# Second gate unit: second-column weight tiles split two tiles ahead into the large pool, with the first nope keys and the second rotary queries

## The chip, the cores and the metric

One core of a Trainium2 chip runs one program. The metric is the device time of one execution in microseconds; the profile has its own execution of the same program, with a row for every instruction of each engine: PE (TensorE, matmuls), DVE (VectorE), ACT (ScalarE), POOL (GpSimd) and SP (SyncE, which issues most of the DMAs).

## The reference

A decoder layer on 512 tokens of width 1024: an input layer norm, then gated linear attention (GLA, four heads) and multi-head latent attention (MLA, eight heads) side by side, merged by gates, and a squared-ReLU MLP of hidden width 4096. All in float32.

```python
q_g, k_g, v_g, r_g, a_lr, q_lat, kv_lat, gate_logits = jnp.split(h @ w_in, offsets, axis=-1)
o_gla = gla_chunked(...); y_gla = (rms_norm(o_gla) * jax.nn.silu(r_g)) @ w_o_gla
q  = (rms_norm(q_lat, q_a_norm_g) @ w_q_b)        # 8 heads: 128 nope and 64 rope columns each
kv = (rms_norm(kv_lat[..., :256], kv_a_norm_g) @ w_kv_b)   # 8 heads: 128 k_nope, 128 v each
y_mla = merge_heads(mla_causal_attention(q_nope, q_rope, k_nope, k_rope, v)) @ w_o_mla
g_gla, g_mla = jnp.split(jax.nn.sigmoid(gate_logits + b_gate), 2, axis=-1)
h = layer_norm(ALPHA * h + (g_gla * y_gla + g_mla * y_mla) @ w_out)
h = layer_norm(ALPHA * h + jnp.square(jax.nn.relu(h @ w_ff1)) @ w_ff2)
```

## The kernel before

**Arithmetic.** A float32 product is made of three fast products: each operand x is split into a rounded high half (`hi`, by ACT, a copy to fp32r) and the rest (`lo = x - hi`, by DVE), and PE computes hi·hi + hi·lo + lo·hi. So each weight tile is loaded raw by DMA (`wraw`, or `wq` for those that are summed first), split, and used as `whi`/`wlo`. The splits have line 111 in the profile, because a helper there issues every ACT and DVE instruction; the matmuls of a unit are lines 1299 to 1301, those of `gemm_fm` 279 to 281, those of `gemm_tm` 313 to 315.

**Units.** The larger products run with seven instead of eight block products. A unit has seven operations: "11", "21" and "22" use a block of the weight as it is, "t1" to "t4" use sums of blocks. `FMO` and `ORDER` list the operations; unit g0 makes the GLA gates, g1 the MLA gates, yg the projection of the GLA output, f1 a part of the MLP. Every operation has two weight tiles, one for each column half g (0 and 1: first and second column), of 128 x 4 x 256 values; each is used by 24 matmuls of 256 columns. The sum t2 is made in place from t1 by adding the raw 22 on DVE (`u_sum`, called by the entry's `post` after the split of 22); t4 is made from t2 by a DMA that adds block 21 into it, issued by POOL (`u_acc`, after the split of t2). The loads of t1 and t3 are two DMAs, a plain one on SP's queue and one that adds on POOL's (`u_load`).

**The stream and its pump.** All weight tiles of the kernel stand in one list, `stream`, in the order in which PE uses them. Ahead of tile i's matmuls the code calls `pump(i)`, which emits loads up to tile i + 2 and splits up to tile i + 1. An entry with `ahead` 2 is split already by `pump(i)` when it is tile i + 2 and everything before it is split:

```python
while st["spl"] < min(len(stream), i + 2 + SPLIT_AHEAD):
    e = stream[st["spl"]]
    if st["spl"] > i + e.get("ahead", SPLIT_AHEAD) and not e["res"]:
        break
    nk, n = e["nk"], e["n"]
    hi, lo = [A([P, nk, T * 2 // nk], F32R, w) for w in HOME["a" if e["res"] else e.get("home", "w")]]
```

`home` says where the halves go: "w" is the pair of tags `whi` and `wlo` with two buffers each; "r" is two buffers of `wraw` (three); "a" is two buffers of the large pool's tag A (names `xh`, `xl`), which has 24 buffers of 4 KB a partition and also holds gate tiles (`gt`, 8), GLA outputs (`ogT`, 8), rotary keys (`KK`), the raw tiles that are summed (`wq`), reloaded latents (`latT`) and head tiles.

**The order around the change.** `GATES` (line 419) runs g0's 11, t1, t2, 22, t3, 21, then g1's 11, g0's t4, and g1's 21, t1, 22, t2, t3, t4. Then come yg's 11, t1, 22, t2, the first rotary queries (qr 0), yg's t3, and head pair 0: nope queries (qn), nope keys (kn), values (mv). After these yg's 21, the second rotary queries (qr 1), yg's t4, and head pairs 1 to 3. `after` asks for yg's t1 tiles once g1's t2 is through, and for its t3 tiles after g1's t3; `after_y` asks for the latents after yg's 11 and 22. Small jobs (GLA heads, row sums `hraw`/`hx`, softmax of the heads) are generators that `tick` advances between matmuls.

**What sets the order.** The program is traced once, in the order of the code. A scheduler then plans each engine's order at build time on a simulated timeline, so an instruction may run ahead of its place in the code when its inputs and a buffer are ready; buffers of one tag are given out in the order of the code, and a request waits until a buffer is free. On the chip each engine and each DMA queue runs its planned order.

Of the kernel before, what the change touches and what calls it, by code (L numbers as in the profile page):

```python
# [52 lines left out]
def tile_hybrid_block(ctx: ExitStack, tc: tile.TileContext, I, out, dbg=None):  # L53
# [115 lines left out]
    stream = []  # L169
# [164 lines left out]
    PL = {}  # L334
# [16 lines left out]
    for op, _ in RW:  # L351
        for hf in range(2):
            PL["r"].append(len(stream))
            e = {"nk": 2, "n": T, "res": False, "ahead": 2, "home": "wwwwrwrwrwwwrw"[2 * RW.index((op, _)) + hf]}
# [24 lines left out]
    def u_src(key, i, j, g):  # L379
        name, c0, gs = UNITS[key]  # L380
        src = I[name].rearrange("(k p) n -> p k n", p=P)
        c0 += (j * gs + g) * 256
        return src[:, i:8:2, c0:c0 + 256]

    def u_sum(key, a, to, g, x, new=None):
        src = WQ[key, (a, g)]
        t = WQ[key, (to, g)] = src if new is None else new
        with tc.issue_after(st["lo"].ins):
            vtt(t, src, x, op=ALU.add)


    def u_acc(key, a, to, g, op):
        t = WQ[key, (to, g)] = WQ[key, (a, g)]
        nc.gpsimd.dma_start(t, u_src(key, int(op[0]) - 1, int(op[1]) - 1, g), accum_op=ALU.add)

    def plan_unit(*seq):
        for key, op in seq:
            for g in range(UNITS[key][2]):
                PL[key, op, g] = len(stream)
                e = {"nk": 4, "n": 256, "res": False}  # L400
                if op[0] != "t" and (op, key) not in HELD:
                    e["dmas"] = [(slice(0, 4), u_src(key, int(op[0]) - 1, int(op[1]) - 1, g), None)]
                else:
                    e["src"] = lambda q=(key, (op, g)): WQ[q]
                    if key == "g0" and op in ("t1", "t2"):
                        e["ahead"], e["home"] = 2, "wr"[g]
                if op == ("t1" if key == "g0" else "22"):
                    e["post"] = lambda raw, q=(key, "t1", "t2", g): u_sum(*q, WQ[q[0], ("22", q[3])] if q[0] == "g0" else raw)
                    if key == "f1":
                        e["post2"] = lambda raw, q=(key, "12", "t3", g): u_sum(*q, raw)  # L410
                elif op == "21" and key == "yg":
                    e["post"] = lambda raw, g=g: u_sum("yg", "t2", "t4", g, raw)
                elif op == "t2" and key == "g1":
                    e["post"] = lambda raw, g=g: u_acc("g1", "t2", "t4", g, "21")
                elif op == "t2" and key != "yg":
                    e["post2" if key == "f1" else "post"] = lambda raw, q=(key, "t2", "t4", g): u_sum(*q, WQ[q[0], ("21", q[3])])
                stream.append(e)

    GATES = [("g0", op) for op in ORDER["g0"][:-1]] + [("g1", "11"), ("g0", "t4")] + [("g1", op) for op, _ in FMO[1:]]
    plan_unit(*GATES)  # L420
    plan_unit(*[("yg", op) for op in ("11", "t1", "22", "t2")])
    plan_qr(0)
    plan_unit(("yg", "t3"))

    def plan_pair(pr):
# [14 lines left out]
    for key in (("ym", 0), ("ym", 1)):  # L440
        for i in PL[key]["idx"]:
            stream[i]["fine"] = True
    stream[PL["ym", 0]["idx"][1]]["late"] = True

    def plan_zip(key, specs):
        pls = [{"idx": [], "nk": 8, "at": []} for _ in specs]
        for k0 in range(0, 8, 2):
            for j, (name, c0, kb, res) in enumerate(specs):
                pl = plan(name, c0, T, kb + k0, kb + k0 + 2, res=res)
                for x in ("idx", "at"):  # L450
                    pls[j][x] += pl[x]
        PL[key] = pls
# [1372 lines left out]
```

## Time and profile before

| | |
|---|---|
| median of 3 runs | 867.83 us (867.54 to 867.85) |
| the profiled execution's own time | 867.63 us |
| its span, first to last instruction | 865.8 us |
| PE busy | 853.8 us, 99% |
| DVE busy | 656.5 us, 76% |
| ACT busy | 491.9 us, 57% |
| POOL busy | 136.5 us, 16% |
| TensorE clock granted | 0.998 of full |
| gate units and yg, window 247 to 330 | PE 82.47 of 83 us |

The page gives busy time by engine, the chain that ended last, and the costliest groups. A row of the timeline is: start in us, length in us, engine, line, operation, output <- inputs (buffer numbers left out), shape, count, and in brackets the idle time before it and what ended that. [...] A row of the DMA view gives the tensor, the issuing queue (SPq, POOLq), the count, KB each, and the median us from issue to landing. A row of the windows gives, after the stretch, its length and the busy time of PE, weight load, DVE, ACT and POOL with their counts, then clock, DMA share and GB/s.

### The profile page before, as it was taken

To read this page: it belongs to the slowest core of one execution; us is meant where nothing else is said; L and a number is where in the kernel's file an instruction comes from. 1 tells how busy PE (TensorE), PEld (TensorE's weight loads), DVE (VectorE), ACT (ScalarE), POOL (GpSimd) and SP (SyncE) were. 2 spreads that over 40 slices of the span, in tenths; PEclk is the share of its full clock that TensorE was granted. 3 is DMA by queue.
4 is the path that set the end of the run, shared out by engine and by line. 5 is a ranking of instruction groups with operands and counts; after the bars stand their busy time and mean duration, and the time that the engine had idled before them with its cause. 6 is when DMAs were issued, how large, how long until landed. Compare 5 with 4: busy or idle time off the path is not lost.

```text
span 865.8 us, 13210 instructions
## 1 busy us (share of the span) xinstructions
PE 853.8 (99%) x4887; PEld 752.8 (87%) x4887; DVE 656.5 (76%) x1141; ACT 491.9 (57%) x863; POOL 136.5 (16%) x179
## 2 busy tenths in 40 slices
PE   8999999999999999999999999999999999999996
PEld 7988888889999998988888889988888888889985
DVE  7857889977578858897856878985567546888865
ACT  6556977655566754565745334475466446766820
POOL 1530001110221103030000021005301520141000
PEclk9999999999999999999999999999999999999999
DMA  9896946696649916233155355009922990499312
GB/s 317 226 199 175 345 148 167 212 264 209 148 148 238 205 43 171 56 104 98 32 176 217 120 167 190 1 1 267 256 61 51 304 214 16 104 243 232 106 69 75
DMA packets 101231, 137.94 MB, mean 159 GB/s; under 512 B 13201, under 2 KB 66116, under 8 KB 101168
## 3 DMA queue, kind: packets, MB, share of 16 engines
q1 hardware_dynamic: 76512, 91.35, 33.6%
q0 software_dynamic: 22784, 41.10, 22.7%
q10 hardware_dynamic: 1872, 4.66, 1.4%
q8 instruction: 38, 0.62, 0.3%
q14 instruction: 25, 0.20, 0.1%
HBM read 113.49 MB, written 8.91 MB: 141 GB/s over the span
## 4 chain that ended last, share of the span: by engine, by line
PE 95%; DVE 3%; ACT 1%; DMA 0%; issue 0%; POOL 0%; POOLq 0%; DVEq 0%
PE mm L279 10%; PE mm L280 10%; PE mm L281 10%; PE mm L1301 6%; PE mm L1299 6%; PE mm L1300 6%; PE mm L314 5%; PE mm L315 5%; PE mm L313 5%; PE px L1633 3%; PE px L1634 3%; PE px L1635 3%; PE mm L1633 2%; PE mm L1634 2%; PE mm L1635 2%; PE mm L863 1%
## 5 line engine op out<-in xcount | busy, mean ns | idle before, releaser
L111 DVE TENSOR_TENSOR wlo<-wraw,whi 128x1024 fp32r<-128x1024 f32 (+2 forms) x96 | 96.0, 1006 | 65.2 <-ACT whi L111 65.1
L111 ACT ACTIVATE whi<-wraw 128x1024 fp32r<-128x1024 f32 (+2 forms) x96 | 84.1, 884 | 77.2 <-PE mm L280 20.7
L111 DVE TENSOR_TENSOR wlo<-wq,whi 128x1024 fp32r<-128x1024 f32 x52 | 63.6, 1223 | 31.9 <-ACT whi L111 31.7
L280 PE MATMUL mm<-h,whi 128*128 128x512 f32 x224 | 87.2, 389 | 0.0
L279 PE MATMUL mm<-h,whi 128*128 128x512 f32 x224 | 87.1, 390 | 0.0
L281 PE MATMUL mm<-h,wlo 128*128 128x512 f32 x224 | 83.2, 390 | 0.0
L111 ACT ACTIVATE whi<-wq 128x1024 fp32r<-128x1024 f32 x52 | 55.0, 1058 | 33.6 <-PE mm L1300 16.1
L1652 POOL DMA_DIRECT2D res<-ev x42 | 38.4, 1064 | 180.7 <-ACT ev L111 150.0
L1301 PE MATMUL mm<-sh,wlo 128*128 128x256 f32 x176 | 50.0, 284 | 0.3 <-DVE wlo L111 0.2
L1299 PE MATMUL mm<-sh,whi 128*128 128x256 f32 x176 | 50.0, 284 | 0.0
L1300 PE MATMUL mm<-sh,whi 128*128 128x256 f32 x176 | 49.8, 283 | 0.0
L279 PEld LDWEIGHTS mm<-h,whi 128*128 128x128 f32 x224 | 42.1, 188 | 8.8
L281 PEld LDWEIGHTS mm<-h,wlo 128*128 128x128 f32 x224 | 42.0, 188 | 8.7
L280 PEld LDWEIGHTS mm<-h,whi 128*128 128x128 f32 x224 | 42.1, 188 | 8.6
L111 ACT ACTIVATE relu<-mm 128x512 f32<-128x512 f32 x26 | 15.2, 594 | 41.9 <-PE mm L281 41.9
L111 ACT ACTIVATE xh<-wraw 128x1024 fp32r<-128x1024 f32 (+1 forms) x24 | 24.1, 1014 | 26.1 <-PE mm L315 15.2
L111 DVE TENSOR_TENSOR xl<-wraw,xh 128x1024 fp32r<-128x1024 f32 (+1 forms) x24 | 27.9, 1171 | 11.8 <-ACT xh L111 11.8
L1301 PEld LDWEIGHTS mm<-sh,wlo 128*128 128x128 f32 x176 | 33.8, 192 | 0.7 <-DVE wlo L111 0.7
L1300 PEld LDWEIGHTS mm<-sh,whi 128*128 128x128 f32 x176 | 33.8, 192 | 0.0
L1299 PEld LDWEIGHTS mm<-sh,whi 128*128 128x128 f32 x176 | 33.8, 192 | 0.0
L1301 PE MATMUL mm<-h,wlo 128*128 128x256 f32 x112 | 32.1, 287 | 0.0
L1299 PE MATMUL mm<-h,whi 128*128 128x256 f32 x112 | 31.8, 284 | 0.0
(487 smaller groups left out, 2784.0 us busy)
## 6 DMA issues: line engine op xcount, KB each, us to landing
wraw<-in_w_ff_dram SPq DMA_DIRECT2D x36, 512.0 KB, 5.0
wraw<-in_w_in_dram SPq DMA_DIRECT2D x30, 512.0 KB, 5.1
wq<-in_w_ff_dram POOLq DMA_DIRECT2D x26, 512.0 KB, 9.4
res<-ev POOLq DMA_DIRECT2D x42, 256.0 KB, 9.9
wq<-in_w_in_dram POOLq DMA_DIRECT2D x20, 512.0 KB, 10.1
wq<-in_w_in_dram SPq DMA_DIRECT2D x18, 512.0 KB, 7.5
hsd<-hs SPq DMA_DIRECT2D x16, 256.0 KB, 3.9
xr<-hsd SPq DMA_DIRECT2D x16, 256.0 KB, 4.3
```

What stands on the lines that cost most here:

```text
L111: ins = op(*a, **k)
L279: mm(o, hi[:, c], xh, start=first, stop=False)
L280: mm(o, hi[:, c], xl, start=False, stop=False)
L281: mm(o, lo[:, c], xh, start=False, stop=last)
L313: mm(o, xh, hi[:, :n], start=opens, stop=False, skip_group_check=share)
L314: mm(o, xh, lo[:, :n], start=False, stop=False, skip_group_check=share)
L315: mm(o, xl, hi[:, :n], start=False, stop=last, skip_group_check=share)
L1299: mm(oa, hi[:, k, c], xh, start=opens and k == 0 and a == 0, stop=False, skip_group_check=True)
L1300: mm(oa, hi[:, k, c], xl, start=False, stop=False, skip_group_check=True)
L1301: mm(oa, lo[:, k, c], xh, start=False, stop=k == 3, skip_group_check=True)
L1633: mm(o, xh[:, c], hi[:, pp], start=opens, stop=False, skip_group_check=True)
L1634: mm(o, xh[:, c], lo[:, pp], start=False, stop=False, skip_group_check=True)
```

## The change

It sets two fields of some entries of `stream`; nothing is computed differently. Every second-column tile of unit g1 (seven entries), the one tile of kn 0 and the two tiles of qr 1 get `ahead` 2 and `home` "a": `pump` emits their splits one tile earlier, and the halves go into two buffers of tag A each in place of the pair `whi`/`wlo`. The `post` of an entry (the sums and the accumulation named above) goes with its split.

```diff
@@ plan_unit, line 404 @@
                     e["src"] = lambda q=(key, (op, g)): WQ[q]
                     if key == "g0" and op in ("t1", "t2"):
                         e["ahead"], e["home"] = 2, "wr"[g]
+                if key == "g1" and g:
+                    e["ahead"], e["home"] = 2, "a"
                 if op == ("t1" if key == "g0" else "22"):
                     e["post"] = lambda raw, q=(key, "t1", "t2", g): u_sum(*q, ...)
@@ after the plans of the head pairs, line 441 @@
             stream[i]["fine"] = True
     stream[PL["ym", 0]["idx"][1]]["late"] = True
+    for key in [("kn", 0), ("qr", 1)]:
+        for i in PL[key]["idx"]:
+            stream[i]["ahead"], stream[i]["home"] = 2, "a"
```

## The prediction

> **What bounds the kernel now.** I read the page first: engine totals, then the chain that ended last.
>
> ```profile
> span 865.8 us, 13210 instructions
> PE 853.8 (99%) x4887; PEld 752.8 (87%) x4887; DVE 656.5 (76%) x1141; ACT 491.9 (57%) x863; POOL 136.5 (16%) x179
> PE 95%; DVE 3%; ACT 1%; DMA 0%; issue 0%; POOL 0%; POOLq 0%; DVEq 0%
> ```
>
> TensorE (PE) is busy 853.8 of 865.8 us and carries 95% of the chain, so splits, loads and evictions cost time only where PE stands still for them. The profiled execution took 867.63 us, 1.8 more than its span; the median of the three runs is 867.83, 0.20 above it. 0.2% of that, 1.74 us, is about what a measurement can tell from no change: faster means under 866.09, slower over 869.57.
>
> Next I read PE's own rows in order of time, because a short stall hides in "busy": a matmul of 256 columns starts every 0.12 us, so a larger step between starts is lost time. These rows surround four such steps in the stretch that the change touches.
>
> ```profile
> 275.90 0.28 PE L1300 MATMUL mm<-sh,whi 128*128 128x256 f32 x1
> 276.33 0.39 PE L1301 MATMUL mm<-sh,wlo 128*128 128x256 f32 x1 [0.15 <-DVE wlo L111]
> 276.55 0.28 PE L1299 MATMUL mm<-sh,whi 128*128 128x256 f32 x1
> ...
> 279.19 0.28 PE L1300 MATMUL mm<-sh,whi 128*128 128x256 f32 x1
> 279.60 0.39 PE L1301 MATMUL mm<-sh,wlo 128*128 128x256 f32 x1
> 279.83 0.28 PE L1299 MATMUL mm<-sh,whi 128*128 128x256 f32 x1
> ...
> 296.85 0.28 PE L1300 MATMUL mm<-ogT,whi 128*128 128x256 f32 x1
> 297.13 0.39 PE L1301 MATMUL mm<-ogT,wlo 128*128 128x256 f32 x1
> 297.35 0.28 PE L1299 MATMUL mm<-ogT,whi 128*128 128x256 f32 x1
> ...
> 338.83 0.40 PE L313 MATMUL mm<-whi,latT 128*128 128x256 f32 x2
> 339.47 0.39 PE L314 MATMUL mm<-wlo,latT 128*128 128x256 f32 x1 [0.25 <-DVE wlo L111]
> 339.69 0.28 PE L315 MATMUL mm<-whi,latT 128*128 128x256 f32 x1
> ```
>
> Each loses the late start and 0.10 at the restart. At 276.33: 276.33 - 275.90 - 0.12 = 0.31, plus 276.55 - 276.33 - 0.12 = 0.10, so 0.41. At 279.60: 0.29 + 0.11 = 0.40. At 297.13: 0.16 + 0.10 = 0.26. At 339.47 the second L313 starts at 338.83 + 0.40 - 0.28 = 338.95, so 0.40 + 0.10 = 0.50. Together 1.57 us, 0.18%. All four wait for a low half (`wlo`). By their order in the code they are: unit g1's tile 22, second column; its tile t2, first column; unit yg's tile 11, first column; the value tile mv of head pair 0.
>
> **The change, step by step.** It adds and removes no instruction and no DMA. It moves ten splits one pump earlier (seven of g1, the one of kn 0, the two of qr 1) and gives them buffers of the large pool (tag A, 24) instead of the two-deep `whi`/`wlo`. A full split costs as before:
>
> ```profile
> 273.02 1.06 ACT L111 ACTIVATE whi<-wraw 128x1024 fp32r<-128x1024 f32 x1 [1.03 <-PE mm L1300]
> 271.24 1.23 DVE L111 TENSOR_TENSOR wlo<-wraw,whi 128x1024 fp32r<-128x1024 f32 x1 [0.98 <-ACT whi L111]
> 272.38 1.22 DVE L111 TENSOR_TENSOR wq<-wq,wraw 128x1024 f32<-128x1024 f32 x1
> 273.85 1.29 DVE L111 TENSOR_TENSOR hraw<-ogT 128x512 f32<-128x512 f32 x2
> 275.05 1.22 DVE L111 TENSOR_TENSOR wlo<-wraw,whi 128x1024 fp32r<-128x1024 f32 x1
> 278.33 1.22 DVE L111 TENSOR_TENSOR wlo<-wq,whi 128x1024 fp32r<-128x1024 f32 x1
> ```
>
> The rows show why PE waited: `whi` at 273.02 started only when PE had left an older tile (its releaser is L1300), and `wlo` stood on VectorE (DVE) behind the sum of 272.38 and the row sums `hraw`. With second columns out of the two-deep pair, a first-column tile no longer waits for the tile just ahead: its buffer was last used two operations earlier, not one. So 22's first column (`wlo` at 271.24) can be split two columns of 24 x 0.12 = 2.88 us earlier, near 265, its sum too, and the DVE work that now piles up between 271 and 280 is spread. The second column of 22 still gets its second A buffer only when PE leaves t1's second column, near 273.0 (what 273.02 waited for); its `wlo` then ends by 273.0 + 1.2 + 1.22 = 275.4 even behind one sum, ahead of 276. I take the whole 0.41 and 0.40. The wait at 297.13 goes with the same buffer rule (yg's first tile inherits a pair that is free one operation sooner): 0.26. Floor for each is zero, if the new order on DVE puts something else ahead. ScalarE (ACT) has the like risk: a `whi` that stands at its head without a buffer would hold the evictions behind it; the order is planned with the buffers known, so I price that at nothing, and at one split, 1.06, if it fails. With t2's split goes the accumulation that makes t4 of it, one pump earlier on POOL's queue and still ahead of yg's; the raw loads on SP's queue follow the earlier releases.
>
> For kn 0 and its neighbour:
>
> ```profile
> 333.80 0.63 ACT L111 ACTIVATE whi<-wraw 128x512 fp32r<-128x512 f32 x1 [1.28 <-PE mm L280]
> 336.12 1.08 ACT L111 ACTIVATE e<-mm 128x512 f32<-128x512 f32 x2
> 337.08 0.65 ACT L111 ACTIVATE whi<-wraw 128x512 fp32r<-128x512 f32 x1
> 338.73 0.68 DVE L111 TENSOR_TENSOR wlo<-wraw,whi 128x512 fp32r<-128x512 f32 x1
> ```
>
> kn's split (333.80) leaves the two-deep pair, so mv's (337.08, the one PE waits for at 339.47) may run some 3 us earlier, before the `e` evictions and what follows them on DVE. Whether it does is a matter of the order planned at build time: between 0 and 0.50, nearer to neither, I take half, 0.25. qr 1's two splits precede no stall now and gain nothing; they ask for four A buffers, which yg's t3 has by then freed (four `ogT` tiles end there), so I cost them at nothing; without those, qr 1 would wait for the pair that kn leaves, as it waits for its raw tile now.
>
> Now what is pushed. A's buffers go out in program order, and the pool is full here. VectorE's split ends and the next request leaves in the same moment:
>
> ```profile
> 283.56 1.23 DVE L111 TENSOR_TENSOR wlo<-wq,whi 128x1024 fp32r<-128x1024 f32 x1 [1.26 <-ACT whi L111]
> 284.81 0.37 SPq L1272 DMA_DIRECT2D wq<-in_w_o_gla_dram  x1
> 286.84 1.22 DVE L111 TENSOR_TENSOR wlo<-wq,whi 128x1024 fp32r<-128x1024 f32 x1
> 288.08 0.34 SPq L1414 DMA_DIRECT2D latT<-latd  x1
> ```
>
> 283.56 + 1.23 = 284.79 and 286.84 + 1.22 = 288.06: both loads on SP's queue waited for a freed `wq`. By the code 21 of the 24 hold key rotary 1, gates 8, `ogT` 8, g1's own sums 4; the other three hold yg's t1 (two) and t3 (one), fetched some 50 us early. Six of g1's seven pairs stand before those requests in program order, so yg's loads, from 250.09 on today (row below), go to somewhere between 281.5 (an estimate: t3's second column split two columns, some 6 us, before its present 286.84 + 1.22) and 284.81, where its last one goes now, and the accumulations on POOL's queue follow them. Their price is in these rows:
>
> ```profile
> 250.09 0.73 SPq L1272 DMA_DIRECT2D wq<-in_w_o_gla_dram  x1
> wq<-in_w_o_gla_dram SPq DMA_DIRECT2D x1, 512.0 KB, 6.3
> wq<-in_w_o_gla_dram POOLq DMA_DIRECT2D x1, 512.0 KB, 6.6
> wq<-in_w_o_gla_dram POOLq DMA_DIRECT2D x1, 512.0 KB, 16.2
> 291.69 1.28 POOL L1274 DMA_DIRECT2D wq<-in_w_o_gla_dram  x1 [8.42 <-DVE hx L111]
> 300.00 1.06 ACT L111 ACTIVATE whi<-wq 128x1024 fp32r<-128x1024 f32 x1
> 302.75 0.28 PE L1299 MATMUL mm<-so,whi 128*128 128x256 f32 x1
> ```
>
> Today the load of 284.81 lands 6.3 later and its accumulation leaves at 291.69, 0.58 after that, and lands in 6.6, at 298.3. The split of t1's first column is due at 300.00 (302.75 on PE). A load at 281.5 gives 281.5 + 6.3 + 0.58 + 6.6 = 295.0, one at 284.8 gives 298.3: both ahead of 299, which is 300 less the first three gains, so the cover is 0.7 to 4 us and I cost the push at nothing. The second t1 column's load may come 3 us later, and PE needs it 2.88 us later. latT, asked for behind them at 288.08 today, is used only after four operations of yg (from 297 on, 5.8 us each), so it has 20 us. g1's own t3 loads wait a few us for a buffer and are split at 283.56 today.
>
> Sum: 0.41 + 0.40 + 0.26 + 0.25 = 1.32. Against the profiled execution 867.63 - 1.32 = 866.31; against the median 867.83 - 1.32 = 866.5.
>
> **The rivals.** First, the pushed tile is late: slower. All of yg's t1 traffic now shares 281 to 305 with g1's t4, latT and yg's t3.
>
> ```profile
> 247.00:281.00 34.00, 33.71 (x279) 33.30 (x278) 26.51 (x36) 21.88 (x35) 7.64 (x6) 1.00 1.03 245
> 281.00:305.00 24.00, 24.00 (x200) 23.80 (x199) 20.82 (x33) 17.66 (x31) 2.69 (x3) 1.00 0.83 186
> ```
>
> The last two columns are DMA share and GB/s. At share 1.03 the accumulation took 16.2 us, at 0.83 it took 6.6. If 281 to 305 saturates too, t1 lands at 281.5 + 6.3 + 0.58 + 16.2 = 304.6, 5.6 after 299: 867.83 - 1.32 + 5.6 = 872.1. It decides from a landing of 10.6 us on (299 - 288.4); from some 13.7 on it eats the gain and 1.74 more. The stretch has spare share and the early loads are half the traffic, hence 0.14. [...]
>
> Second, nothing moves: the pool is full, so a second-column pair waits for the pair before it, and only `whi` runs ahead. If DVE still reaches the two `wlo` late, only 0.26 or less is left: 867.6. For it: 21 of 24 buffers taken. Against it: the first columns gain depth without any A buffer. Chance 0.22.
>
> Third, more goes than these four. The largest other stall behind them:
>
> ```profile
> 326.15 0.39 PE L1299 MATMUL mm<-ogT,whi 128*128 128x256 f32 x1 [0.24 <-ACT whi L111]
> 372.71 0.47 PE L279 MATMUL mm<-latT,whi 128*128 128x512 f32 x1 [0.58 <-ACT PT L111]
> ```
>
> With the 0.58 of 372.71, the 0.24 of 326.15 and all of mv's 0.50 the gain is 1.57 + 0.82 = 2.39: 865.4. Against it: both hang on PE's own progress (a `whi` buffer, a softmax transpose). Chance 0.14.
>
> **How the numbers follow.** My forecast has 0.50, its own range 866.0 (all of mv's 0.50 and a little more) to 867.2 (one of the two 0.4 stays, mv's too); late tile 0.14, nothing 0.22, more 0.14. Faster: 0.14 and 0.04 of the forecast, 0.18. Slower: 0.13 of the late tile. Same: 0.69. The range runs from the third rival, 865.3, to the middle of the late tile (2.8 late: 869.3), 869.5.
>
> **What would show it.** Right: no step over 0.12 at g1's 22 and t2 and yg's 11; `xh`/`xl` rows in that stretch; `whi` of 22's first column near 265; yg's t1 loads after 280. Wrong: PE waiting at yg's t1 for `whi` behind a DMA; new gaps where evictions stand behind early splits; head scores starting later after 342.

## The result and the profile after

| | before | after |
|---|---|---|
| median of 6 runs | 867.77 us (867.54 to 867.96) | 871.44 us (871.23 to 871.78) |
| ratio to before | | 1.0043, 95% interval 1.003 to 1.0056 |
| profiled execution, its span | 867.63, 865.8 us | 871.78, 870.0 us |

The kernel became 3.7 us slower, outside the range of the prediction (865.3 to 869.5). The page of the changed kernel, its span, its engines and its chain:

```profile
span 870.0 us, 13196 instructions
PE 856.0 (98%) x4887; PEld 755.0 (87%) x4887; DVE 656.4 (75%) x1141; ACT 492.1 (57%) x863; POOL 136.6 (16%) x179
PE 93%; DVE 2%; DMA 2%; ACT 1%; issue 1%; POOL 0%; POOLq 0%; DVEq 0%; SPq 0%; ACTq 0%
```

The work is the same (4887 matmuls), PE's share of the chain fell from 95% to 93%, and DMA went from 0% to 2%: somewhere the end now hangs on a transfer. PE itself is busy 2.2 us longer with the same matmuls. Both are followed below. The unit's matmuls are now lines 1304 to 1306.

PE's new standstills between 280 and 350 us, in order of time, with the row ahead of each:

```profile
284.55 0.28 PE L1306 MATMUL mm<-sh,xl 128*128 128x256 f32 x1
285.29 0.38 PE L1304 MATMUL mm<-sh,whi 128*128 128x256 f32 x1 [0.46 <-ACT u L111]
...
291.02 0.28 PE L1306 MATMUL mm<-sh,xl 128*128 128x256 f32 x1
293.64 0.58 PE L1304 MATMUL mm<-ogT,whi 128*128 128x256 f32 x1 [2.34 <-ACT whi L111]
294.02 0.41 PE L1305 MATMUL mm<-ogT,whi 128*128 128x256 f32 x1
294.24 0.41 PE L1304 MATMUL mm<-h,whi 128*128 128x256 f32 x1
294.45 0.41 PE L1305 MATMUL mm<-h,whi 128*128 128x256 f32 x1
...
345.40 0.28 PE L315 MATMUL mm<-whi,latT 128*128 128x256 f32 x1
346.13 0.39 PE L1304 MATMUL mm<-ogT,whi 128*128 128x256 f32 x1 [0.46 <-ACT whi L111]
346.36 0.28 PE L1305 MATMUL mm<-ogT,whi 128*128 128x256 f32 x1
347.39 0.38 PE L1306 MATMUL mm<-ogT,wlo 128*128 128x256 f32 x1 [0.76 <-DVE wlo L111]
```

Against a step of 0.12 the standstills cost, with 0.10 for each restart: 0.62 + 0.10 = 0.72 at 285.29 (g1's t3, first column), 2.50 + 0.26 = 2.76 at 293.64 (yg's 11, first column; the 0.26 holds the low clock of which more below), 0.61 + 0.10 = 0.71 at 346.13 and 0.92 + 0.10 = 1.02 at 347.39 (yg's 21, first column).

What ACT did ahead of the first two of these:

```profile
283.17 1.06 ACT L111 ACTIVATE whi<-wq 128x1024 fp32r<-128x1024 f32 x1 [2.26 <-DMA wq<-in_w_in_dram]
284.65 0.58 ACT L111 ACTIVATE u<-mm 128x512 f32<-128x512 f32 x1
...
290.79 1.06 ACT L111 ACTIVATE xh<-wq 128x1024 fp32r<-128x1024 f32 x1 [4.03 <-DMA wq<-in_w_in_dram]
291.75 0.89 ACT L111 ACTIVATE gt<-u,hbg 128x256 f32<-128x256 f32 x2
292.55 1.04 ACT L111 ACTIVATE whi<-wraw 128x1024 fp32r<-128x1024 f32 x1
```

The row of 290.79 is the split of g1's t4, second column, now two tiles ahead and into the pool (`xh`). It stood at ACT's head for 4.03 us until POOL's accumulation had landed, at 290.76. Behind it stood two gate evictions and, at 292.55, the split of yg's 11, for which PE waited at 293.64. In the same way t4's first column (283.17) waited 2.26 us, and with it the eviction `u` at 284.65 that PE's 285.29 needed.

DVE was held in the same way. The low half of t4's second column waited 2.72 us for ACT's `xh`, and behind it stood the eviction `e` of t3, which must leave its bank before PE can add t4's first column to it:

```profile
291.88 1.23 DVE L111 TENSOR_TENSOR xl<-wq,xh 128x1024 fp32r<-128x1024 f32 x1 [2.72 <-ACT xh L111]
293.02 0.68 DVE L111 TENSOR_TENSOR e<-e,mm 128x512 f32<-128x512 f32 x1
```

So PE could not have gone on with t4 in place of yg's 11 before 293.70 either; in kernels 1 and 7 below it waits (1.02 and 1.54 us) for an `e` that stands behind such a low half.

Before, the second accumulation left POOL at 281.99 and landed at 289.88, and the two t4 splits, 288.23 and 291.10, waited for no DMA:

```profile
279.21 1.06 ACT L111 ACTIVATE whi<-wq 128x1024 fp32r<-128x1024 f32 x1 [0.34 <-PE mm L1300]
280.47 1.22 DVE L111 TENSOR_TENSOR wlo<-wq,whi 128x1024 fp32r<-128x1024 f32 x1
281.99 1.28 POOL L394 DMA_DIRECT2D wq<-in_w_in_dram  x1 [0.86 <-DVE wlo L111]
288.23 1.06 ACT L111 ACTIVATE whi<-wq 128x1024 fp32r<-128x1024 f32 x1 [0.59 <-ACT gt L111]
291.10 1.06 ACT L111 ACTIVATE whi<-wq 128x1024 fp32r<-128x1024 f32 x1
```

The rows of 279.21 and 280.47 are the high and the low half of t2's second column. In the changed kernel, the same two halves and the accumulation that waits for them:

```profile
275.68 1.06 ACT L111 ACTIVATE xh<-wq 128x1024 fp32r<-128x1024 f32 x1 [1.37 <-DVE wq L111]
280.38 2.35 DVE L111 TENSOR_TENSOR xl<-wq,xh 128x1024 fp32r<-128x1024 f32 x2
282.40 1.30 POOL L394 DMA_DIRECT2D wq<-in_w_in_dram  x1 [4.05 <-issue]
```

So t4's second split was planned earlier while its input came no earlier: the accumulation of that column may only start when t2's low half is made, and DVE reached that half (280.38, the first of the two) 4.7 us after the high half of 275.68. The high half moved 3.5 us ahead, the low half 0.09. The accumulation left at 282.40, against 281.99 before, and landed 8.36 us after its issue, against 7.89.

The standstill has a second price. The windows give the granted clock behind DVE's, ACT's and POOL's columns, ahead of DMA share and GB/s:

```profile
293.00:294.00 1.00, 0.36 (x1) 0.36 (x2) 1.00 (x4) 1.00 (x3) 0.60 (x1) 0.81 0.75 117
294.00:295.00 1.00, 1.00 (x6) 1.00 (x6) 1.00 (x3) 1.00 (x3) 0.00 (x0) 0.50 0.65 154
...
297.00:298.00 1.00, 1.00 (x10) 1.00 (x10) 1.00 (x3) 0.57 (x2) 0.00 (x0) 0.99 1.07 201
```

As PE resumed, its clock went to 0.50 and stayed there for 3.4 us (293.61 to 297.02). The matmuls follow each other by 0.21 us (294.02, 294.24, 294.45 above) in place of 0.12: 14 such steps from 294.02 to 297.01, 2.99 - 14 x 0.12 = 1.31 us.

Sum for the profiled execution: 0.72 + 2.76 + 1.31 + 0.71 + 1.02 = 6.52 lost. Gained: 0.41 + 0.40 + 0.26 + 0.50, the prediction's four, and 0.74 ahead of 372.71, together 2.31. Net 4.21; measured 871.78 - 867.63 = 4.15.

### The profile page after: what moved, and what is told of

Same layout as the page of the kernel before. It is cut to its first block, busy times and chain, and to the rows that moved or that the text cites. A ratio compares the mean times of both kernels' runs of the same rounds, so it can differ in the third digit from the quotient of the medians.

```text
span 870.0 us, 13196 instructions
## 1 busy us (share of the span) xinstructions
PE 856.0 (98%) x4887; PEld 755.0 (87%) x4887; DVE 656.4 (75%) x1141; ACT 492.1 (57%) x863; POOL 136.6 (16%) x179
## 4 chain that ended last, share of the span: by engine, by line
PE 93%; DVE 2%; DMA 2%; ACT 1%; issue 1%; POOL 0%; POOLq 0%; DVEq 0%; SPq 0%; ACTq 0%
PE mm L279 10%; PE mm L280 10%; PE mm L281 10%; PE mm L1304 5%; PE mm L1306 5%; PE mm L1305 5%; PE mm L314 5%; PE mm L315 5%; PE mm L313 5%; PE px L1638 3%; PE px L1639 3%; PE px L1640 2%; PE mm L1638 2%; PE mm L1639 2%; PE mm L1640 2%; PE mm L866 1%
## 5 line engine op out<-in xcount | busy, mean ns | idle before, releaser
L111 DVE TENSOR_TENSOR wlo<-wraw,whi 128x1024 fp32r<-128x1024 f32 (+2 forms) x90 | 90.5, 1012 | 64.9 <-ACT whi L111 64.7
L111 ACT ACTIVATE whi<-wraw 128x1024 fp32r<-128x1024 f32 (+2 forms) x90 | 79.2, 888 | 70.1 <-PE mm L280 20.8
L111 DVE TENSOR_TENSOR wlo<-wq,whi 128x1024 fp32r<-128x1024 f32 x48 | 58.7, 1223 | 30.3 <-ACT whi L111 30.0
L111 ACT ACTIVATE whi<-wq 128x1024 fp32r<-128x1024 f32 x48 | 50.7, 1057 | 30.9 <-PE mm L1305 18.6
L111 ACT ACTIVATE xh<-wraw 128x1024 fp32r<-128x1024 f32 (+3 forms) x30 | 29.0, 973 | 30.4 <-PE mm L315 15.3
L111 DVE TENSOR_TENSOR xl<-wraw,xh 128x1024 fp32r<-128x1024 f32 (+3 forms) x30 | 33.4, 1119 | 13.8 <-ACT xh L111 12.8
L1304 PE MATMUL mm<-sh,whi 128*128 128x256 f32 x144 | 41.0, 285 | 0.5 <-ACT u L111 0.5
L1306 PE MATMUL mm<-sh,wlo 128*128 128x256 f32 x144 | 40.7, 283 | 0.0
L1305 PE MATMUL mm<-sh,whi 128*128 128x256 f32 x144 | 40.7, 283 | 0.0
L1304 PEld LDWEIGHTS mm<-sh,whi 128*128 128x128 f32 x144 | 27.6, 192 | 0.7 <-ACT u L111 0.7
L1304 PE MATMUL mm<-h,whi 128*128 128x256 f32 x96 | 27.9, 291 | 0.0
L1305 PE MATMUL mm<-h,whi 128*128 128x256 f32 x96 | 27.7, 289 | 0.0
L1305 PEld LDWEIGHTS mm<-sh,whi 128*128 128x128 f32 x144 | 27.6, 192 | 0.0
```

The source lines that it names most:

```text
L111: ins = op(*a, **k)
L1304: mm(oa, hi[:, k, c], xh, start=opens and k == 0 and a == 0, stop=False, skip_group_check=True)
L1305: mm(oa, hi[:, k, c], xl, start=False, stop=False, skip_group_check=True)
L1306: mm(oa, lo[:, k, c], xh, start=False, stop=k == 3, skip_group_check=True)
```

## The experiments

All are compared with before on the same chip (its medians there: 867.76 for the first four, 867.70 for the next four, 867.75 for the last). "The change" is the whole change. The edits are shown against the changed kernel, at the two places that the change touches; "no heads" stands for an empty list of kn 0 and qr 1 in the second place.

| kernel | median (us), lowest to highest | ratio to before, 95% |
|---|---|---|
| 1 all but t4 | 869.98, 868.81 to 871.73 | 1.0029, 1.0019 to 1.004 |
| 2 all but qr 1 | 873.93, 872.38 to 874.56 | 1.0069, 1.0055 to 1.0082 |
| 3 g1 alone | 871.68, 869.91 to 871.88 | 1.004, 1.0028 to 1.0053 |
| 4 kn 0 and qr 1 alone | 867.72, 867.18 to 868.90 | 1.000, 0.9991 to 1.0009 |
| 5 gap filled, 18 matmuls | 869.91, 869.28 to 870.87 | 1.0025, 1.0015 to 1.0034 |
| 6 t4 in the pool, one ahead | 868.01, 867.06 to 871.42 | 1.0005, 0.9997 to 1.0014 |
| 7 t4 alone | 872.41, 871.96 to 873.47 | 1.0052, 1.0039 to 1.0066 |
| 8 tile 22 alone | 868.20, 868.05 to 869.62 | 1.0008, 0.9999 to 1.0017 |
| 9 g1 alone, t4 one ahead | 867.69, 867.39 to 868.65 | 0.9999, 0.999 to 1.0007 |
| 10 as 9, t4's first split held | 867.96, 867.47 to 869.06 | 1.0003, 0.9994 to 1.0012 |
| 11 gap filled, 9 matmuls | 870.52, 870.22 to 871.09 | 1.0033, 1.002 to 1.0046 |
| 12 qr 1 alone | 867.00, 866.56 to 868.01 | 0.9992, 0.9984 to 1.0001 |

### The order on ACT: t4 (1, 6, 7)

All but t4's second column:

```diff
-                if key == "g1" and g:
+                if key == "g1" and g and op != "t4":
```

> Everything of the change but g1's tile t4, second column, which is split one tile ahead into the pair whi/wlo as before. Theory A (a split planned early stands at ACT's head until POOL's accumulation has landed, and the gate evictions and yg 11's whi stand behind it): in the plan of this kernel two gt evictions now go ahead of that split, and PE has t4's second column before yg 11, so PE's 2.76 us at 293.64 go: 871.44 - 2.76 = 868.7 (868.2 to 869.2). The 0.72 at 285.29 stays, because t4's first column keeps its place. Rival B (the pool is to blame: yg's t1 loads, pushed from 250 to 282.76, slow the accumulation and whatever comes there): those loads are still pushed by the six other tiles, so the time stays at 871.4 (870.9 to 871.9).

869.98, between the two theories. ACT's row for t4's second column is now behind the first two gate evictions, but it still waited 3.83 us:

```profile
291.89 1.06 ACT L111 ACTIVATE whi<-wq 128x1024 fp32r<-128x1024 f32 x1 [3.83 <-DMA wq<-in_w_in_dram]
295.29 0.36 PE L1304 MATMUL mm<-h,whi 128*128 128x256 f32 x1 [1.02 <-DVE e L111]
```

The accumulation left at 282.38 and let ACT go at 291.89, 9.5 us later; the loads of yg, which SP issued from 282.73 on, flew beside it. PE lost 1.18 at 295.29 and 0.66 at 299.14 in place of 2.50 at once; the clock stayed at 1.00 in the profiled execution. Two of the eight executions took 871.6 and 871.7; what their clock did there is not on record. So the place of this one split is not all: what waits for the late accumulation pays in either order, only less.

The same split into the pool, so that the loads are pushed as before, but emitted one tile ahead:

```diff
-                    e["ahead"], e["home"] = 2, "a"
+                    e["ahead"], e["home"] = 1 + (op != "t4"), "a"
```

> The whole change, but g1's tile t4, second column, is emitted one tile ahead and not two; it still goes into two pool buffers, so yg's loads are pushed as in the change. In the plan yg 11's first split and the gt evictions now stand ahead of t4's split. Theory A (order on ACT): the step of 2.76 at 293.64 goes, and with it the low clock's 1.7: 871.44 - 4.46 = 867.0 (866.4 to 868.0); the steps at 285.29 and at yg 21 stay. Rival B (the accumulation, slowed by the pushed loads, is late for whatever waits on it): PE waits for t4's second column instead, some 2 us later in the order: 870 to 871.9.

868.01, at the upper end of theory A and 3.4 below the change. The split of yg's 11 now stands ahead of t4's:

```profile
288.50 1.06 ACT L111 ACTIVATE whi<-wraw 128x1024 fp32r<-128x1024 f32 x1 [0.42 <-ACT gt L111]
291.25 0.28 PE L1304 MATMUL mm<-ogT,whi 128*128 128x256 f32 x1
291.38 1.06 ACT L111 ACTIVATE xh<-wq 128x1024 fp32r<-128x1024 f32 x1
```

t4's second split (291.38) waits for no DMA any more, and PE goes from t3 into yg's 11 (291.25) without a step. The accumulation landed at 290.95, as late as in the change (290.76): what differs is only what stood behind the wait. One number, 2 or 1, decides over 3.4 us.

The other way round, t4's second column alone:

```diff
-                if key == "g1" and g:
+                if key == "g1" and g and op == "t4":
...
-    for key in [("kn", 0), ("qr", 1)]:
+    for key in []:
```

> Only g1's tile t4, second column, two tiles ahead in the pool; every other tile as before the change. One pair does not push yg's t1 loads from 250 to 282. Theory A: in the plan this split stands ahead of two gt evictions and of t4's first split; the accumulation issued near 282 lands near 289, so t4's first split starts near 291 instead of 288.23 and PE waits some 1.2 us: 867.77 + 1.2 = 869.0, and 870.7 where the clock falls as well (868.4 to 871.0). Rival B (without pushed loads the accumulation is there in time): 867.8 (867.4 to 868.2).

872.41: worse than the whole change, and above even theory A's range. One pair of the pool and one tile of lead lose 4.7 us:

```profile
289.91 1.06 ACT L111 ACTIVATE xh<-wq 128x1024 fp32r<-128x1024 f32 x1 [2.77 <-DMA wq<-in_w_in_dram]
291.68 1.04 ACT L111 ACTIVATE whi<-wq 128x1024 fp32r<-128x1024 f32 x1
292.98 0.36 PE L1304 MATMUL mm<-h,whi 128*128 128x256 f32 x1 [1.54 <-DVE e L111]
294.82 0.58 PE L1304 MATMUL mm<-ogT,whi 128*128 128x256 f32 x1 [1.37 <-ACT whi L111]
```

Behind the waiting `xh` stood both the first column of t4 (291.68; 288.23 before) and, at 293.73, yg's 11, and PE stood still twice, 1.70 and 1.53 us; the clock was at 0.50 from 293.8 to 300.6. Yg's t1 loads had left from 250.40 on, as before the change: that the pushed loads are needed for the loss is refuted.

### The clock (5, 11)

The whole change with 18 extra matmuls, whose product the first matmul of yg's 11 overwrites:

```diff
-                    xh, xl = ops[k][ph]
+                    xh, xl = ops[k][ph]; [mm(o[:, :256], xh[:, :128], xh, start=True, stop=True, skip_group_check=True) for _ in range(18 if (key, op, g, k) == ("yg", "11", 0, 0) else 0)]
```

> The whole change, and 18 extra matmuls of 128x256 on PE right ahead of yg 11's first column, into the bank that this column clears anyway: 18 x 0.12 = 2.16 us of work that stands in the queue where PE stood still for 2.50 us. Theory C (the stall costs twice: itself, and the 3.4 us at half clock that follow it, 293.61 to 297.02 in the trace after, worth 1.7): the clock stays at 1.00 after 293 and the time falls although PE has more to do: 871.44 - 1.7 = 869.7 (869.3 to 870.2). Rival (the low clock has another cause, such as the load of the DMA queues or a fixed point of time): the clock falls again and the time stays at 871.4 or above (871.2 to 871.9).

869.91: PE does 2.2 us more and the kernel ends 1.5 us sooner.

```profile
294.00:295.00 1.00, 1.00 (x10) 1.00 (x10) 1.00 (x2) 1.00 (x4) 0.00 (x0) 1.00 0.64 108
```

The same window of the changed kernel is shown above: the DMA share is the same there (0.65; in the 6 us from 287 to 293 it was 1.20 there and 1.19 here), but here the clock is 1.00 and 10 matmuls fall in the window, not 6. With PE kept busy the clock stayed at 1.00 at the same time and DMA share (0.64).

With 9 in place of 18:

> The whole change with 9 extra matmuls (1.08 us) where 18 stood in the filled gap: some 1.5 us of the standstill are left. Theory C (the length of the standstill decides whether the clock halves): between the filled gap's 869.9 and 871.4. If 1.5 us never halve the clock: 869.9 (869.3 to 870.3); if they do so in some executions, single times fall in two groups 1.7 apart, 869.9 and 871.6; if they always do, 871.6.

870.52, between, and the single times (870.22 to 871.09) form no two groups. The standstill left over did not halve the clock:

```profile
293.57 0.38 PE L1304 MATMUL mm<-ogT,whi 128*128 128x256 f32 x1 [1.27 <-ACT whi L111]
```

```profile
294.00:295.00 1.00, 1.00 (x11) 1.00 (x10) 1.00 (x2) 1.00 (x3) 0.00 (x0) 1.00 0.59 140
```

Behind 1.43 us lost the clock is 1.00. The plan behind had moved too (yg's 21 lost 1.14 + 0.92 in this kernel), so that 870.52 can't be compared to better than some tenths.

### g1 without and with its parts (3, 8, 9, 10)

g1 alone, no heads (`for key in []:` in the second place):

> Only the seven second-column tiles of g1; kn 0 and qr 1 as before. Theory A: as without qr 1, and the step of 0.50 that PE lost at mv 0 before is back if kn 0's pair was what took it: 869.7 + 0.5 = 870.2 (869.6 to 870.6). If mv 0's step went by itself with what g1 moves: 869.7. Rival B (all of the loss comes from g1's pool buffers): 871.4 + 0.5 = 871.9.

871.68, 1.5 above theory A's figure and near rival B's: the net loss is g1's. The single steps are nevertheless as theory A has them: those at yg 21 were gone, mv 0's 0.41 + 0.10 was back, and so was the 0.74 ahead of 372.71, which the expectation had left out. Four of the five executions took 871.2 to 871.9. The profiled one took 869.91: it has the standstill (2.36 us lost at 293.51), but a clock of 1.00 behind it:

```profile
293.51 0.39 PE L1304 MATMUL mm<-ogT,whi 128*128 128x256 f32 x1 [2.20 <-ACT whi L111]
293.60:297.00 3.40, 3.40 (x29) 3.40 (x30) 3.40 (x8) 2.76 (x8) 0.00 (x0) 1.00 0.74 160
```

The other four were 1.3 to 2.0 longer. That this is the halved clock is not shown, since they have no trace; it is near the 1.3 to 1.5 that the low clock cost in the change.

Tile 22's second column alone (`and op == "22"` in the first place, and no heads):

> Only g1's tile 22, second column, two tiles ahead in the pool, all else as before: no split is moved ahead of an accumulation. The prediction's first step: PE's steps of 0.41 at 276.33 and 0.40 at 279.60 go, and nothing comes for them: 867.77 - 0.8 = 867.0 (866.6 to 867.4). Rival (the low halves on VectorE stand behind something else as soon as one moves): 867.8 (867.4 to 868.4).

868.20, a miss. The two steps of 0.4 went, and yg 11's 0.26, but a new one came:

```profile
264.95 1.06 ACT L111 ACTIVATE xh<-wraw 128x1024 fp32r<-128x1024 f32 x1 [1.55 <-DMA wraw<-in_w_in_dram]
265.91 1.04 ACT L111 ACTIVATE whi<-wq 128x1024 fp32r<-128x1024 f32 x1
268.45 0.38 PE L1306 MATMUL mm<-sh,wlo 128*128 128x256 f32 x1 [0.81 <-DVE wlo L111]
```

The early split of 22 stands at ACT's head for its raw tile (1.55 us), ahead of t1's first split (265.91; 264.34 before), and PE loses 0.97 at t1. It is the t4 pattern with a plain load.

g1 alone with t4 one tile ahead (the edits of 6 and 3 together):

> Only the seven tiles of g1, and t4 of them emitted one tile ahead and not two; kn 0 and qr 1 as before. Theory A (each step has one cause in the order on ScalarE): of the 868.0 of the same kernel with kn 0 and qr 1, the two steps at yg 21 go (0.70 + 1.02) and the steps that kn 0 and qr 1 took come back (0.50 at mv 0, 0.74 ahead of yg's t4): 868.0 - 1.7 + 1.2 = 867.5 (867.0 to 868.0). Rival B (the pushed loads of yg still cost): 868.0 to 869.0.

867.69, as theory A has it, and no different from before: the three steps gained are paid back by 0.56 at 285.08 (the `u` eviction) and by this:

```profile
303.68 1.06 ACT L111 ACTIVATE whi<-wq 128x1024 fp32r<-128x1024 f32 x1 [0.80 <-DMA wq<-in_w_o_gla_dram]
306.05 0.39 PE L1306 MATMUL mm<-so,wlo 128*128 128x256 f32 x1 [0.31 <-DVE wlo L111]
```

Here are yg's pushed t1 tiles: both splits wait for their accumulation (2.38 us the first, 0.80 the second, shown), and PE loses 0.46 + 0.11 at yg's t1.

The same, with t4's first split held behind the `u` evictions:

```diff
-                    act(u2[g], o, AF.Copy)
+                    st["u"] = act(u2[g], o, AF.Copy); stream[PL["g1", "t4", 0]].update({"gates": (st["u"],)} if key == "g1" else {})
```

> As the kernel with g1 alone and t4 late, and the split of t4's first column may not be issued before the eviction of t2's second column, so that in the plan both u evictions stand ahead of it. Theory A: PE's step of 0.72 at 285.29, which waits for the first u eviction behind that split, goes: 867.5 - 0.7 = 866.8 (866.3 to 867.3). Rival (the bank is late for another reason): 867.5 (867.0 to 868.0).

The step at 285 went, as theory A has it (matmuls at 284.71, 284.83 and 284.95 follow without a gap), but the time did not fall: 867.96. The yg t1 tile grew later by nearly as much:

```profile
304.07 1.06 ACT L111 ACTIVATE whi<-wq 128x1024 fp32r<-128x1024 f32 x1 [1.45 <-DMA wq<-in_w_o_gla_dram]
```

PE now loses 0.92 + 0.10 at yg's t1. With the order mended, what follows from the loads pushed to 282 is late next.

### The heads (2, 4, 12)

In the changed kernel the first split of qr 1 stood ahead of yg 21's two:

```profile
344.72 0.42 ACT L111 ACTIVATE xh<-wraw 128x256 fp32r<-128x256 f32 x1 [1.95 <-DMA wraw<-in_w_q_b_dram]
345.04 1.04 ACT L111 ACTIVATE whi<-wraw 128x1024 fp32r<-128x1024 f32 x1
```

All but qr 1 (`[("kn", 0)]`):

> Everything of the change but qr 1. Theory A (qr 1's first split stands at ACT's head for 1.95 us for its raw tile, ahead of yg 21's two splits and a qn eviction): PE's two steps at yg 21, 0.71 at 346.13 and 1.02 at 347.39, go: 871.44 - 1.73 = 869.7 (869.3 to 870.1). Rival B (yg 21's raw tiles come 1.6 to 3.5 us later than before, because SP's queue or the buffers are behind after the 3.85 lost earlier, and qr 1 has no part in it): 871.4 (871.0 to 871.8).

873.93, 2.5 more than the change: a miss on both sides. The steps at yg 21 did go, but in this plan both splits of yg's t4 (355.08 and 357.37 on ACT; 351.13 and 354.92 in the change) come right ahead of the softmax of head pair 0, and PE waits for that softmax. That these splits make it late is read from the order of the rows and was not tested:

```profile
361.21 0.33 PE L1133 MATMUL px<-ca,P 128*128 128x128 f32 x1 [1.48 <-DVE P L111]
```

```profile
363.00:364.00 1.00, 1.00 (x6) 1.00 (x6) 1.00 (x7) 0.80 (x2) 0.00 (x0) 0.50 0.00 0
```

1.64 us lost, and behind it the half clock a second time, from 362.2 to 365.6, now with no DMA in flight.

kn 0 and qr 1 alone, g1 as before (a condition that no entry meets, `and op == "none"`, in the first place):

> Only kn 0 and qr 1; g1 as before. Theory A: 867.77 - 0.50 (mv 0's step) + 1.73 (yg 21's steps) = 869.0 (868.3 to 869.5). Rival B (heads are harmless, g1 alone loses): 867.77 - 0.50 = 867.3 (866.9 to 867.8). Together with g1 alone the two changes from before should add to the 3.67 us of the whole change within 0.5 if the parts do not meet.

867.72, within rival B's range, but not for its reason. The steps of theory A came (0.56 + 0.10 and 0.92 + 0.10 at yg 21), mv 0's 0.51 went, and so did the 0.74 ahead of 372.71, which theory A had not counted: 1.7 lost against 1.3 gained, and the medians do not differ. With g1 alone at +3.92 and the heads at -0.04 the parts add to 3.9, near the whole's 3.67.

qr 1 alone (`[("qr", 1)]`, g1 as before):

> Only qr 1's two splits, all else as before. Theory A: in the plan its first split now stands ahead of yg 21's second split, and its second one ahead of yg t4's second split, each waiting for its raw tile: one step of 0.5 to 1.0 at yg 21, nothing gained, 868.2 to 868.8; with 1.7 more if the clock halves. Rival (qr 1 alone is harmless; yg 21's steps belong to kn 0): 867.7 (867.4 to 868.0).

867.00, a miss for both: the lowest of all, 0.75 below before, with an interval (0.9984 to 1.0001) that reaches no change by a hair. In this plan qr 1's first split stands behind yg 21's first and ahead of its second:

```profile
343.48 0.42 ACT L111 ACTIVATE xh<-wraw 128x256 fp32r<-128x256 f32 x1 [2.63 <-DMA wraw<-in_w_q_b_dram]
372.33 0.47 PE L279 MATMUL mm<-latT,whi 128*128 128x512 f32 x1
```

It waits longer than in the changed kernel, 2.63 us, and costs nothing, since yg 21's second split has time until then. And the row of 372.33 has no wait, where 372.71 had one of 0.58 before. That step of 0.74 is the only one gone and as large as the gain; why the plan of the heads turns out better there was not taken apart.

## Why the prediction was wrong

Point by point, by its own steps:

- The four standstills of `wlo` went, as forecast, mv 0's 0.50 whole and not half; so did the third rival's 372.71, while its 326.15 stayed (330.20, with the same 0.24). The gain was 2.31 and not 1.32. Its signs came too: 22's second low half at 273.28 (forecast by 275.4 at its end), no step at 276 and 279.
- Yg's t1 loads went to 282.76, inside the forecast 281.5 to 284.81. The first rival, that they come late, did not set this kernel's time: t1's first accumulation landed at 294.32, ahead even of the forecast's 295.0, and the split of 304.59 waits for no DMA. In kernels 6, 9 and 10, without the standstill, the rival is there, at 0.4 to 1.0 us and not 5.6. All four loads of yg left by 288.6 in them (two only from 293.1 on in the change), and t1's two accumulations took 9.6 to 11.3 us (6.2 and 8.9 in the change): the prediction's cover of 0.7 to 4 us was spent.
- The step that failed: "a `whi` that stands at its head without a buffer would hold the evictions behind it; the order is planned with the buffers known, so I price that at nothing, and at one split, 1.06, if it fails." The mechanism was named and then looked for in the wrong resource. Not a buffer was missing but the data: a split that is planned ahead of a DMA's landing. The next sentence, that t4's accumulation goes "one pump earlier on POOL's queue", was wrong for the second column: 282.40 for 281.99, because t2's low half on DVE, on which it waits, did not move with the high half. The wait was 4.03 us on ACT and 2.76 on PE, not 1.06. Kernel 6 shows that this step cost most of the time: with t4 one tile ahead the same kernel takes 868.01.
- Not in the sum at all: the clock, 1.31 in the profile; 1.5 by the filled gap.
- qr 1, "I cost them at nothing": beside kn 0, 1.7 us at yg 21; alone, a gain. Its cost is not its own but that of the order that the plan gives the whole stretch.

What stays open: the order of the heads that makes kernel 2 lose and qr 1 alone gain.

## What to carry to other kernels

When a split is moved ahead, ask when its input lands and not only when its buffer is free: ACT ran its planned order here, so the split that waited 4.03 us for a DMA (290.79) held two gate evictions and yg 11's split (292.55) behind it, and PE, which needed that split next, paid 2.76 us. An input that is itself made by a step of the moved chain (here a low half, then an accumulation of 8.36 us) moves only as far as its slowest link. Price a long standstill of PE with the clock behind it: here one of 2.50 us brought another 1.31 us in the profile, 1.5 by the filled gap, and one of 2.36 in kernel 3's profiled execution brought none.

## What the runs showed of the hardware

The granted clock of PE went to 0.50 for about 3.4 us with a standstill of 2.50 us (the change; low from 293.61 to 297.02), with one of 2.43 (kernel 2 at 293.64; low from 293.96 to 297.4) and with one of 1.64 (kernel 2 at 361.21; low from 362.2 to 365.6). In kernel 7, with standstills of 1.70 that ended at 292.98 and of 1.53 that ended at 294.82, it was at 0.50 from 293.8 to 300.6, 6.8 us. It stayed at 1.00 behind 1.43 (kernel 11), 1.18 (kernel 1) and 2.36 (kernel 3's profiled execution). So the length of a single standstill does not tell these cases apart: 2.36 passed where 1.64 did not. Why was not shown, and neither was what brings the clock back.

An accumulating DMA of 512 KB let its reader go 7.6 us after its issue at 282.29 in kernel 7 and 9.5 after its issue at 282.38 in kernel 1, where SP's loads of yg started at 282.73 beside it. In the change, where two of these loads started from 282.76 on, it was 8.4; what else adds to the difference was not separated.
